# Scan beside two projections: sums moved to the transposes, relus ordered behind a cast, row loads and input parts put later

## The chip, the cores and the metric

The kernel runs on one core of one Trainium2 chip. TensorE (PE) multiplies matrices, VectorE (DVE) and ScalarE (ACT) work on vectors, GpSimd (POOL) does a little copying, and SyncE (SP) issues nearly all DMA transfers from one queue, in order. The metric is the device time of one execution in microseconds. Three runs of the kernel before the change took 2610.78 to 2611.7 us, median 2611.38.

## The reference

One layer of a hybrid encoder over 2048 frames of width 1024. Two mixers read the same normalised input. One is a short gated convolution; the other is a chunked state-space scan (SSD), with 16 heads of 64 in two groups and a state of 128. Both feed one output projection, then comes a squared-ReLU MLP and a last norm. What the change touches is the scan and the output projection:

```python
def ssd_scan(xs, dt, a_head, bm, cm):
    ...
    x_c = (xs.astype(f32) * dt[..., None]).reshape(b, nc, CHUNK, g, r, p)
    a_c = (dt * a_head).reshape(b, nc, CHUNK, g, r)
    a_cum = jnp.cumsum(a_c, axis=2)
    seg = a_cum[:, :, :, None] - a_cum[:, :, None, :]
    decay = jnp.exp(jnp.where(causal[None, None, :, :, None, None], seg, -jnp.inf))
    scores = jnp.einsum("bclgn,bcsgn->bclsg", c_c, b_c)
    y_diag = jnp.einsum("bclsgr,bcsgrp->bclgrp", scores[..., None] * decay, x_c)
    decay_end = jnp.exp(a_cum[:, :, -1:] - a_cum)
    states = jnp.einsum("bclgn,bclgrp->bcgrpn", b_c, x_c * decay_end[..., None])
    chunk_decay = jnp.exp(a_cum[:, :, -1])

    def step(hs, inp):
        s_c, d_c = inp
        return hs * d_c[..., None, None] + s_c, hs
    ...
    y_off = jnp.einsum("bclgn,bcgrpn->bclgrp", c_c, prev) * jnp.exp(a_cum)[..., None]
    return (y_diag + y_off).reshape(b, t, h, p)

def ssd_mixer(z, xbc, dt_raw, conv_w, conv_b, dt_bias, a_log, d_skip, norm_w):
    ...
    y = ssd_scan(xs, dt, a_head, bm, cm)
    y = y + d_skip.astype(jnp.float32)[:, None] * xs.astype(jnp.float32)
    y = y.reshape(b, t, SSD_INNER).astype(z.dtype)
    gated = (y * jax.nn.silu(z)).reshape(b, t, SSD_GROUPS, SSD_INNER // SSD_GROUPS)
    gated = rmsnorm(gated, norm_w.reshape(SSD_GROUPS, SSD_INNER // SSD_GROUPS))
    return gated.reshape(b, t, SSD_INNER)
    ...
    y = jnp.concatenate([y_a, y_b], axis=-1)
    x = x + jnp.einsum("btc,cd->btd", y, w_out)
```

## The kernel before

Every large product is made of three matmuls (whi by hi, whi by lo, wlo by hi): each operand is split into a rounded part (a cast on ACT) and the remainder (a subtraction on DVE). The input projection runs over two halves of 1024 frames, in pairs of column blocks, each pair as a chain of seven products (lines 246 to 290; the accumulators px, py and pw). The output projection (class Output) runs in 64 units, each one column block of 128 by one block of 512 frames, 24 matmuls into pm.

The scan takes 32 chunks of 128 frames (4 blocks, 2 groups, 4 chunks each) and is no loop of its own. It is a generator (`run`) that gives way after each step, and the projections advance it. In the first stage (16 chunks, one buffer of most tiles) one step runs after each of the seven products of the second half of the input projection. In the second stage (16 chunks, two buffers) it runs from the units of the output projection: one step in the middle of a unit, two at its end.

The work of a chunk n is in two generators.

- `front(n)`, first part: PE transposes x (ptx, L1449) and B (ptb, L1452) and multiplies B with C (L1453). ACT copies xtok (L1455) and casts btok (L1437). DVE makes xdt, masks the scores (smask) and weights xtok, and from that come the two parts of xde: the cast on ACT (L1437) and the subtraction on DVE (L1438). Second part: eight relus, one a head, over the rows dec (L1469), one exp (L1470), four multiplications of xd by the skip weight (L1472), all on ACT. Third part: DVE multiplies dec with the masked scores (L1474).
- `back(n)`, first part: PE forms the new state contribution st from btok and xde (mm3, L114 to L116), yo from the state (L1490), yd from dec and xdt (L1493). DVE updates the state (L1509, L1510) and adds yo times eb and yd (L1511, L1512). Second part: the skip term and the gate (L1514, L1515). Third: squares and their sums (ssq). Fourth: one product sums over the partitions (pss, L1524), then a square root on ACT and a reciprocal. Fifth: the scaled result is stored.

The rows come by DMA: `load(n)` fetches B and C (bc), x (xd) and dec, `load_rows(n)` fetches eb, `load_gate(n)` the gate y. dec is read by yd of the same buffer's earlier chunk, so its load waits for that product. In a chunk of the first stage nine steps are traced, in the second eight; which part stands in which step is written out by hand in `run`.

The scheduler that turns the program into queues takes instructions by program order as a priority, yet lets a later one go first where it thinks that its inputs are there earlier. `tc.issue_after` (in the helper `behind`, L100) fixes the order of two instructions of one engine; it puts no wait on the chip. PSUM banks go by tags: tp has two, yo, yd and mw one each, mm three.

In `Output`, `residual(n)` fetches the block of x to which unit n is added (xt, three buffers), and `fill` splits the inputs of the projection, for those from the scan (i = 1) with a weight (L1628 on ACT, L1629 on DVE).

Of the kernel before, what the change touches and what calls it, by code (L numbers as in the profile page):

```python
# [21 lines left out]
L = 128  # L22
# [17 lines left out]
def trunk(ctx: ExitStack, tc: tile.TileContext, x, x_tok, w_in, w_dt, w_out, w_up, w_down, cvec, hrow, out):  # L40
# [1321 lines left out]
    class Scan:  # L1362
# [5 lines left out]
        def open(self, stack, name, bufs):  # L1368
            self.sp = stack.enter_context(tc.tile_pool(name=name, bufs=1, reuse_waits="tile"))
            self.bufs = bufs  # L1370
            self.got = {}

        def tile(self, shape, tag, bufs=None):
# [10 lines left out]
        def load(self, n):  # L1384

            if n >= self.end:
                return
            b, g, c, h, ts, r0 = self.place(n)
            t = self.got[n] = {}
            if (g, c) == (0, 0) or n == self.begin:  # L1390
                dd = self.tile([4, NC * 16], "dd")
                nc.sync.dma_start(dd, dt_d[b])
                self.dd = {**getattr(self, "dd", {}), b: dd}
            t["dd"] = dd = self.dd[b]
            bc = t["bc"] = self.tile([2, L], "bc", 2)
            for i in range(2):
                nc.sync.dma_start(bc[:, i], xs_d[h][:, 8 + 2 * i + g, ts])
            t["xd"] = self.tile([4, L], "xd")
            nc.sync.dma_start(t["xd"], xs_d[h][:, 4 * g : 4 * g + 4, ts])
            t["dec"] = self.tile([HG, L], "dec")  # L1400
            nc.sync.dma_start(t["dec"], rd_d[b][r0 : r0 + HG, 0, :].partition_broadcast(P))
            three = lambda i: dd[:, i].rearrange("p (c h) -> p c h", c=NC)[:, c, g * HG : (g + 1) * HG]
            heads = lambda a: a.unsqueeze(2).to_broadcast([P, HG, 64])
            t["dt"], t["cdec"], t["dend"] = heads(three(0)), heads(three(2)), heads(three(3))
            t["a"] = dd[:, 1, r0 : r0 + HG]
            t["first"], t["last"] = (b, c) == (0, 0), (b, c) == (NB - 1, NC - 1)

        def load_rows(self, n):
# [24 lines left out]
        def pieces(self, shape, tag, src):  # L1433

            pair = self.sp.tile([P] + shape, F32R, tag=tag, name=tag, bufs=1)
            hi, lo = pair[:, 0], pair[:, 1]
            nc.scalar.copy(hi, src)  # L1437
            nc.vector.tensor_tensor(out=lo, in0=src, in1=hi.bitcast(F32), op=ALU.subtract)  # L1438
            return hi, lo

        def front(self, n):
# [12 lines left out]
            xtok = self.tile([512], "xtok", 1)  # L1454
            nc.scalar.copy(xtok, pt)  # L1455
            if not t["last"]:
                t["btok"] = self.pieces([2, P], "btok", pb[:, 0:P])
            sm = self.tile([L], "smask", 1)
            nc.vector.tensor_tensor(out=sm, in0=pb[:, P : 2 * P], in1=tri, op=ALU.mult)
# [7 lines left out]
            dec = t["dec"]  # L1467
            for i in range(HG):
                nc.scalar.activation(dec[:, i], dec[:, i], AF.Relu, bias=t["a"][:, i : i + 1], scale=-1.0)  # L1469
            nc.scalar.activation(dec, dec, AF.Exp, scale=-1.0)  # L1470
# [6 lines left out]
        def back(self, n):  # L1477
# [29 lines left out]
            else:  # L1507
                if not t["last"]:
                    nc.vector.tensor_tensor(out=byhead(state), in0=byhead(state), in1=t["cdec"], op=ALU.mult)  # L1509
                    nc.vector.tensor_tensor(out=state, in0=state, in1=st, op=ALU.add)  # L1510
                nc.vector.tensor_tensor(out=t1, in0=yo, in1=t["eb"].rearrange("p j l -> p (j l)"), op=ALU.mult)  # L1511
# [10 lines left out]
            yield  # L1522
            pss = psum("tp", "pss", 2) if self.bufs == 1 else psum("mw", "pss", accs["mw"])
            nc.tensor.matmul(pss[:, 0:L], ones, ssq, start=True, stop=True)  # L1524
# [8 lines left out]
        def run(self, begin, end):  # L1533

            self.begin, self.end = begin, end
            for n in range(begin, begin + self.bufs):
                self.load(n)
                self.load_gate(n)
                self.load_rows(n)
            yield  # L1540
            front = self.front(begin)
            for _ in front:
                yield
            if self.bufs == 1:
                for n in range(begin, end):
                    back = self.back(n)
                    front = self.front(n + 1) if n + 1 < end else iter(())
                    next(back)
                    yield
                    next(back)  # L1550
                    self.load(n + 1)
                    self.load_rows(n + 1)
                    yield
                    next(back)
                    yield
                    yield
                    next(front, None)
                    yield
                    next(back)
                    yield  # L1560
# [9 lines left out]
            for n in range(begin, end):  # L1570
# [3 lines left out]
                yield  # L1574
                next(before, None)
                yield
                next(back)
                self.load(n + 2)
                self.load_rows(n + 2)
                yield  # L1580
                next(front, None)
                yield
                if next(before, "end") != "end":
# [13 lines left out]
    class Output:  # L1597
# [19 lines left out]
        def fill(self, i, b, c, k, t):  # L1617

            blk = self.y.setdefault((i, b), {})
            for n in range(2):  # L1620
# [5 lines left out]
                if i:  # L1626
                    w = col(C_NSSD, f)
                    nc.scalar.mul(hi, o, w)  # L1628
                    nc.vector.scalar_tensor_tensor(out=lo, in0=o, scalar=w, in1=r, op0=ALU.mult, op1=ALU.subtract)  # L1629
                else:  # L1630
# [50 lines left out]
        def unit(self, n, hook):  # L1681

            i, b, d = self.UNITS[n]
            self.residual(n + 1)
            if n % 2:
# [3 lines left out]
            for k in range(KD):  # L1689
                if k == KD // 2:  # L1690
                    hook(2 * n)
                mm3(pm, whi[:, k, :], wlo[:, k, :], *self.y[i, b][k], k, KD)
            t = self.xt.pop(n)
# [179 lines left out]
```

## Time and profile before

| | |
|---|---|
| median of three runs | 2611.38 us |
| the profiled execution | 2612.25 us |
| its span, first to last instruction | 2610.1 us |
| mean granted TensorE clock | 0.998 |
| DVE busy, ACT busy | 73%, 55% |
| DMA | 533.55 MB, mean 204 GB/s |

The profile is one execution. Its rows name a line, an engine, an operation and the tiles (out<-in). A matmul's duration is longer than its share of PE's time, since matmuls overlap: from start to start a product of 512 columns takes 0.23 us. In a timeline the square bracket tells how long the engine stood still before the row and what ended that. The view of waits sums, for pairs of a waiting instruction and what released it, the microseconds, the number of times and the longest. A view of stretches gives the busy time of each engine between two times and the granted clock there.

### The profile page before, as it was taken

To read this page: it belongs to the slowest core of one execution; us is meant where nothing else is said; L and a number is where in the kernel's file an instruction comes from. 1 tells how busy PE (TensorE), PEld (TensorE's weight loads), DVE (VectorE), ACT (ScalarE), POOL (GpSimd) and SP (SyncE) were. 2 spreads that over 40 slices of the span, in tenths; PEclk is the share of its full clock that TensorE was granted. 3 is DMA by queue.
4 is the path that set the end of the run, shared out by engine and by line. 5 is a ranking of instruction groups with operands and counts; after the bars stand their busy time and mean duration, and the time that the engine had idled before them with its cause. 6 is when DMAs were issued, how large, how long until landed. Compare 5 with 4: busy or idle time off the path is not lost.

```text
span 2610.1 us, 33626 instructions
## 1 busy us (share of the span) xinstructions
PE 2591.5 (99%) x12067; PEld 2134.8 (82%) x12067; DVE 1909.7 (73%) x2625; ACT 1432.2 (55%) x2185; POOL 59.0 (2%) x98
## 2 busy tenths in 40 slices
PE   9999999999999999999999999999999999999998
PEld 7888888788888888888888888888888888888887
DVE  7988666677778777877767765755558877876875
ACT  7553345876667676766326555655456444444443
POOL 0000000000000000000000000000000000000001
PEclk9999999999999999999999999999999999999999
DMA  5657435555555488876665674643448766676872
GB/s 214 206 201 253 183 145 182 180 159 168 184 163 169 140 276 276 274 229 211 204 210 210 230 274 142 244 167 140 163 142 283 265 202 206 225 238 214 282 246 77
DMA packets 289559, 533.55 MB, mean 204 GB/s; under 512 B 25840, under 2 KB 141552, under 8 KB 289392
## 3 DMA queue, kind: packets, MB, share of 16 engines
q1 hardware_dynamic: 288816, 530.88, 60.4%
q8 instruction: 94, 1.54, 0.2%
q14 instruction: 73, 0.60, 0.1%
q10 hardware_dynamic: 576, 0.52, 0.1%
HBM read 354.63 MB, written 176.69 MB: 204 GB/s over the span
## 4 chain that ended last, share of the span: by engine, by line
PE 65%; issue 25%; DVE 4%; DMA 3%; ACT 2%; SPq 0%; POOL 0%; POOLq 0%; DVEq 0%; ACTq 0%
PE px L271 9%; PE px L273 9%; PE px L272 9%; PE py L271 5%; PE py L273 5%; PE py L272 5%; PE pm L114 4%; PE pm L116 4%; PE pm L115 4%; PE pw L271 2%; PE pw L272 2%; PE pw L273 2%; PE pm L466 1%; PE yd L1493 1%; DMA dec<-rd_d 1%
## 5 line engine op out<-in xcount | busy, mean ns | idle before, releaser
L271 PE MATMUL px<-uh,whi 128*128 128x512 f32 x1672 | 655.6, 392 | 3.8 <-DVE e L982 1.2
L273 PE MATMUL px<-uh,wlo 128*128 128x512 f32 x1672 | 651.7, 390 | 0.0
L272 PE MATMUL px<-ul,whi 128*128 128x512 f32 x1672 | 651.7, 390 | 0.0
L271 PEld LDWEIGHTS px<-uh,whi 128*128 128x128 f32 x1672 | 314.0, 188 | 74.0 <-DVE acc L1182 3.2
L273 PEld LDWEIGHTS px<-uh,wlo 128*128 128x128 f32 x1672 | 314.0, 188 | 65.6 <-issue 0.2
L106 DVE TENSOR_TENSOR wlo<-wraw,whi 128x1024 fp32r<-128x1024 f32 (+2 forms) x224 | 226.9, 1013 | 191.1 <-ACT whi L105 190.7
L272 PEld LDWEIGHTS px<-ul,whi 128*128 128x128 f32 x1672 | 314.1, 188 | 63.8
L105 ACT CAST whi<-wraw 128x1024 fp32r<-128x1024 f32 (+2 forms) x224 | 197.7, 882 | 277.6 <-PE px L272 211.1
L105 ACT CAST whi<-s 128x1024 fp32r<-128x1024 f32 (+1 forms) x206 | 215.3, 1045 | 227.8 <-PE py L272 92.5
L271 PE MATMUL py<-uh,whi 128*128 128x512 f32 x836 | 327.0, 391 | 0.0
L272 PE MATMUL py<-ul,whi 128*128 128x512 f32 x836 | 325.8, 390 | 0.0
L273 PE MATMUL py<-uh,wlo 128*128 128x512 f32 x836 | 325.8, 390 | 0.0
L106 DVE TENSOR_TENSOR wlo<-s,whi 128x1024 fp32r<-128x1024 f32 (+1 forms) x206 | 250.5, 1216 | 76.2 <-ACT whi L105 74.9
L114 PE MATMUL pm<-uh,whi 128*128 128x512 f32 (+1 forms) x584 | 226.8, 388 | 0.0
L116 PE MATMUL pm<-uh,wlo 128*128 128x512 f32 (+1 forms) x584 | 223.4, 383 | 0.0
L115 PE MATMUL pm<-ul,whi 128*128 128x512 f32 (+1 forms) x584 | 223.1, 382 | 0.0
L271 PEld LDWEIGHTS py<-uh,whi 128*128 128x128 f32 x836 | 157.0, 188 | 32.8 <-issue 0.5
L273 PEld LDWEIGHTS py<-uh,wlo 128*128 128x128 f32 x836 | 157.0, 188 | 32.6
L272 PEld LDWEIGHTS py<-ul,whi 128*128 128x128 f32 x836 | 157.1, 188 | 32.2
L326 DVE TENSOR_TENSOR ul<-rh,uh 128x1024 fp32r<-128x1024 f32 (+1 forms) x128 | 138.9, 1088 | 48.3 <-ACT uh L325 48.0
L325 ACT CAST uh<-rh 128x1024 fp32r<-128x1024 f32 (+1 forms) x128 | 119.9, 942 | 94.4 <-PE py L273 61.1
L271 PE MATMUL pw<-uh,whi 128*128 128x512 f32 x418 | 163.4, 391 | 0.0
(250 smaller groups left out, 3834.0 us busy)
## 6 DMA issues: line engine op xcount, KB each, us to landing
hid_d<-e SPq DMA_DIRECT2D x96, 512.0 KB, 4.2
rh<-hid_d SPq DMA_DIRECT2D x96, 512.0 KB, 4.6
wraw<-w_in SPq DMA_DIRECT2D x67, 512.0 KB, 4.0
wraw<-w_up SPq DMA_DIRECT2D x62, 512.0 KB, 4.3
wraw<-w_down SPq DMA_DIRECT2D x88, 256.0 KB, 4.2
dec<-rd_d SPq DMA_DIRECT2D x32, 512.0 KB, 5.4
wraw<-w_out SPq DMA_DIRECT2D x32, 512.0 KB, 4.8
x_d<-xt SPq DMA_DIRECT2D x64, 256.0 KB, 3.6
```

What stands on the lines that cost most here:

```text
L105: nc.scalar.copy(hi, raw)
L106: eng.tensor_tensor(out=lo, in0=raw, in1=hi.bitcast(F32), op=ALU.subtract)
L114: nc.tensor.matmul(out, whi, hi, start=(k == 0), stop=False)
L115: nc.tensor.matmul(out, whi, lo, start=False, stop=False)
L116: nc.tensor.matmul(out, wlo, hi, start=False, stop=(k == nk - 1))
L271: nc.tensor.matmul(p, hi, h[0], start=bool(first and k == 0), stop=False, **kw)
L272: nc.tensor.matmul(p, hi, h[1], start=False, stop=False, **kw)
L273: nc.tensor.matmul(p, lo, h[0], start=False, stop=(k == len(g) - 1), **kw)
L325: nc.scalar.copy(p[i][0], t)
L326: nc.vector.tensor_tensor(out=p[i][1], in0=t, in1=p[i][0].bitcast(F32), op=ALU.subtract)
L466: last[engine] = make(*args, **kw).ins
L1493: nc.tensor.matmul(yd[(i % 2) * 64 : (i % 2) * 64 + 64, (i // 2) * L : (i // 2 + 1) * L], byhead(t["xdt"])[:, i, :], t["dec"][:, i, :], st ...
```

## The change

In both stages the sum over the partitions (fourth part of `back`) is traced directly ahead of the transposes of the next front; in the first stage its bank is yo's and no longer one of tp's. The relus of a front are ordered behind the last cast of the front before (btok's, or the copy of xtok where there is none). The loads of a chunk are traced one step earlier; in the first stage that of x stays where it was, as a step of its own (`load_x`). In the second stage the front's first part comes a step earlier, and the first row loads (eb) stand behind the first front. In the output projection the residual of the next unit is fetched in the middle of a unit and no longer at its start, and the lower parts of the scan's outputs are ordered behind the state update traced last.

```diff
         def open(self, stack, name, bufs):
...
             self.got = {}
+            self.copied = self.updated = None
...
-            t["xd"] = self.tile([4, L], "xd")
-            nc.sync.dma_start(t["xd"], xs_d[h][:, 4 * g : 4 * g + 4, ts])
+            if self.bufs > 1 or n == self.begin:
+                self.load_x(n)
...
+        def load_x(self, n):
+
+            if n < self.end:
+                b, g, c, h, ts, r0 = self.place(n)
+                x = self.got[n]["xd"] = self.tile([4, L], "xd")
+                nc.sync.dma_start(x, xs_d[h][:, 4 * g : 4 * g + 4, ts])
...
         def pieces(self, shape, tag, src):
...
-            nc.scalar.copy(hi, src)
+            self.cast = nc.scalar.copy(hi, src).ins
...
         def front(self, n):
...
-            nc.scalar.copy(xtok, pt)
+            last, self.copied = self.copied, nc.scalar.copy(xtok, pt).ins
             if not t["last"]:
                 t["btok"] = self.pieces([2, P], "btok", pb[:, 0:P])
+                self.copied = self.cast
...
-            for i in range(HG):
-                nc.scalar.activation(dec[:, i], dec[:, i], AF.Relu, bias=t["a"][:, i : i + 1], scale=-1.0)
+            with behind(last):
+                for i in range(HG):
+                    nc.scalar.activation(dec[:, i], dec[:, i], AF.Relu, bias=t["a"][:, i : i + 1], scale=-1.0)
...
         def back(self, n):
...
-                    nc.vector.tensor_tensor(out=state, in0=state, in1=st, op=ALU.add)
+                    self.updated = nc.vector.tensor_tensor(out=state, in0=state, in1=st, op=ALU.add).ins
...
-            pss = psum("tp", "pss", 2) if self.bufs == 1 else psum("mw", "pss", accs["mw"])
+            pss = psum("yo", "pss") if self.bufs == 1 else psum("mw", "pss", accs["mw"])
...
         def run(self, begin, end):
...
-                self.load_rows(n)
+                if self.bufs == 1:
+                    self.load_rows(n)
             yield
             front = self.front(begin)
+            next(front)
+            if self.bufs > 1:
+                for n in range(begin, begin + self.bufs):
+                    self.load_rows(n)
+            yield
             for _ in front:
                 yield
             if self.bufs == 1:
...
                     next(back)
-                    yield
-                    next(back)
                     self.load(n + 1)
                     self.load_rows(n + 1)
                     yield
                     next(back)
+                    self.load_x(n + 1)
+                    yield
+                    next(back)
                     yield
                     yield
+                    next(back)
                     next(front, None)
                     yield
-                    next(back)
                     yield
                     next(front, None)
                     yield
...
                 next(back)
                 yield
-                next(before, None)
-                yield
                 next(back)
                 self.load(n + 2)
                 self.load_rows(n + 2)
                 yield
+                next(before, None)
                 next(front, None)
+                yield
                 yield
                 if next(before, "end") != "end":
                     self.load_gate(n + 1)
...
         def fill(self, i, b, c, k, t):
...
-                    nc.vector.scalar_tensor_tensor(out=lo, in0=o, scalar=w, in1=r, op0=ALU.mult, op1=ALU.subtract)
+                    with behind(scan.updated):
+                        nc.vector.scalar_tensor_tensor(
+                            out=lo, in0=o, scalar=w, in1=r, op0=ALU.mult, op1=ALU.subtract
+                        )
...
         def unit(self, n, hook):
 
             i, b, d = self.UNITS[n]
-            self.residual(n + 1)
             if n % 2:
                 self.split_weights()
...
                 if k == KD // 2:
                     hook(2 * n)
+                    self.residual(n + 1)
                 mm3(pm, whi[:, k, :], wlo[:, k, :], *self.y[i, b][k], k, KD)
```

## The prediction

> **What bounds the kernel now.** I read the page first, then the view of stretches over the two stages in which the scan runs, then the waits of TensorE (PE) there, and last the timelines around those waits.
>
> ```profile
> PE 2591.5 (99%) x12067; PEld 2134.8 (82%) x12067; DVE 1909.7 (73%) x2625; ACT 1432.2 (55%) x2185; POOL 59.0 (2%) x98
> ```
>
> PE is busy 99% of the span, and the change neither adds nor removes a matmul. So it can only win back time in which PE waits, and only between 450 and 1260 us, where the scan runs beside the projections.
>
> ```profile
> 450.00:947.00 497.00, 495.58 (x2478) 405.18 (x2477) 379.82 (x543) 348.72 (x586) 19.28 (x40) 1.00 0.55 174
> 947.00:1100.00 153.00, 153.00 (x827) 126.68 (x826) 115.96 (x185) 101.10 (x206) 0.00 (x0) 1.00 0.90 282
> 1100.00:1130.00 30.00, 28.61 (x152) 22.84 (x152) 20.42 (x33) 21.05 (x42) 0.00 (x0) 1.00 0.77 239
> 1198.00:1208.00 10.00, 8.00 (x43) 6.19 (x42) 8.58 (x16) 6.41 (x9) 0.00 (x0) 0.83 0.79 263
> ```
>
> Each row gives the stretch, its length, and the busy time of PE, its weight loads, DVE, ACT and POOL with their instructions, then the granted clock. In the first stage (450 to 947) PE stands still 1.42 us. In the second it stands still 1.39 us between 1100 and 1130 and 2.00 us between 1198 and 1208, where the granted clock is 0.83 besides; from 947 to 1100 it never does. These idle times are short of the true loss, since a busy PE can also be a slow one, so I take starts of matmuls. First a chunk that nothing disturbs, then the three disturbed ones:
>
> ```profile
> 1087.14 0.40 PE L116 MATMUL pm<-uh,wlo 128*128 128x512 f32 x1
> ...
> 1087.61 0.48 PE L115 MATMUL st<-xde,btok 128*128 128x512 f32 x1
> ...
> 1089.14 1.09 PE L1493 MATMUL yd<-dec,stmp 128*64 128x128 f32 x16
> 1090.16 0.50 PE L114 MATMUL pm<-uh,whi 128*128 128x512 f32 x1
> ```
>
> ```profile
> 1104.78 0.39 PE L116 MATMUL pm<-uh,wlo 128*128 128x512 f32 x1
> 1105.51 0.51 PE L114 MATMUL st<-xde,btok 128*128 128x512 f32 x1 [0.35 <-ACT xde L1437]
> ...
> 1109.23 0.50 PE L114 MATMUL pm<-uh,whi 128*128 128x512 f32 x1
> ```
>
> ```profile
> 1126.56 0.39 PE L116 MATMUL pm<-uh,wlo 128*128 128x512 f32 x1
> ...
> 1129.42 1.09 PE L1493 MATMUL yd<-dec,stmp 128*64 128x128 f32 x16
> ```
>
> ```profile
> 1199.47 0.39 PE L116 MATMUL pm<-uh,wlo 128*128 128x512 f32 x1
> 1201.62 0.49 PE L114 MATMUL st<-xde,btok 128*128 128x512 f32 x1 [1.77 <-ACT xde L1437]
> 1202.35 0.79 PE L115 MATMUL st<-xde,btok 128*128 128x512 f32 x1 [0.23 <-DVE xde L1438]
> ...
> 1206.42 0.50 PE L114 MATMUL pm<-uh,whi 128*128 128x512 f32 x1
> ```
>
> From the last product before the chunk (pm L116) to the first one behind it the undisturbed chunk takes 3.02 us, and 2.00 us to its yd. The others take 4.45 (1.43 lost), 2.86 to yd (0.86 lost) and 6.95 (3.93 lost): **6.22 us**. Each waits for the cast of xde on ScalarE (ACT). Why is that late?
>
> ```profile
> 1100.46 1.57 ACT L1469 ACTIVATE dec<-dec,dd 128x128 f32<-128x128 f32 x5 [6.64 <-DMA dec<-rd_d]
> ...
> 1102.23 0.57 ACT L1455 COPY xtok<-ptx 128x512 f32<-128x512 f32 x1
> ...
> 1104.85 0.61 ACT L1437 CAST xde<-xtok 128x512 fp32r<-128x512 f32 x1
> ```
>
> ```profile
> 1193.39 2.45 ACT L1469 ACTIVATE dec<-dec,dd 128x128 f32<-128x128 f32 x8 [5.41 <-DMA dec<-rd_d]
> ...
> 1200.97 0.60 ACT L1437 CAST xde<-xtok 128x512 fp32r<-128x512 f32 x1
> ```
>
> Counted from the start of the scan, eight relus a chunk, the relus here belong to the chunk after the one whose transposed inputs are copied (xtok) and cast (xde). They are ahead in ACT's queue and wait 6.64 and 5.41 us for rows (dec) that have not landed, while the transposes have long been done (1096.03, quoted below). Everything behind them on ACT is late by that.
>
> **The change part by part.**
>
> *Relus behind the cast of the chunk ahead.* The edge joins two ACT instructions, so it adds no wait, only an order: xtok and btok go ahead of the relus. Queued behind the relus stay their own exp, the cast of xde and the weight casts; DVE's subtraction for xde waits for that cast, and PE's st for both.
>
> ```profile
> L1438 DVE TENSOR_TENSOR xde<-xtok,xde 128x512 fp32r<-128x512 f32 x30 | 20.4, 681 | 3.4 <-ACT xde L1437 3.2
> ```
>
> The copy at 1102.23 can now run at about 1096.8, right behind the transposes. What can still be late is xde alone: rows at 1100.46, eight relus of 2.45, the cast of 0.61 and the subtraction of 0.68 give 1104.2; st L115 is due undisturbed at 1105.2 (1104.78 plus two products of 0.23; 1087.14 to 1087.61 holds two such). With other ACT work between, up to the 4.39 that passed from 1100.46 to 1104.85 in place of 2.45, it would be 0.9 late; I count **+0.4** between the ends 0 and 0.9. At 1199 the same sum gives 1197.2 against 1199.7. What is late next is nothing on PE. All three stalls go: **-6.2**.
>
> *Front a step earlier in the second stage.* Steps are spread over half units of twelve products (2.8 us), so transposes of two chunks in three come 2.8 us earlier and none later: more room for the same chain, no price of its own.
>
> *Sums (pss) beside the transposes.* Does a group of small matmuls cost more alone than joined?
>
> ```profile
> 1093.03 0.38 PE L1524 MATMUL pss<-ssq,ones_r 128*128 128x128 f32 x2
> ...
> 1093.48 0.40 PE L115 MATMUL pm<-ul,whi 128*128 128x512 f32 x1
> ```
>
> ```profile
> 1096.03 0.60 PE L1449 MATMUL ptx<-ident,xd 128*128 128x128 f32 x4
> ...
> 1097.03 0.39 PE L115 MATMUL pm<-ul,whi 128*128 128x512 f32 x1
> ```
>
> Less the one product of 0.23 in each stretch, two matmuls of pss cost 0.22 alone and the seven of the transposes 0.77: 0.11 each both times. So joining them is worth **0**. Against that stands only the 0.48 that the first product behind a group shows instead of 0.39; were that a price per group, 32 groups would give 2.9, which I keep as the end of the range.
>
> *The first stage's sums in bank yo.*
>
> ```profile
> ACT dec L1469 <- DMA dec<-rd_d: 51.4, 21, 6.6
> ...
> PEld ptx L1449 <- DMA xd<-xs_d: 0.8, 2, 0.4
> ...
> PEld pss L1524 <- ACT xtok L1455: 0.7, 2, 0.5
> ```
>
> Their wait for a bank (0.7 in weight loads) falls away: **-0.2**, bounds 0 and -0.7. The new wait is for DVE's product of yo, four steps (11 us) earlier in program order; queued behind the waiting pss on PE would stand the transposes and all products. The next chunk's yo in turn waits for the square root, again four steps on. Were a sum itself late, one step (2.8) is the price; no row shows PE waiting for ssq.
>
> *Input parts behind the state; residual half a unit later; row loads behind the first front; loads a step earlier.* The lower input parts (DVE) now follow the state update that was traced last; behind them stand weight parts and additions, and the first products that read them come units later. The residual load:
>
> ```profile
> L1667 SPq DMA_DIRECT2D xt<-x x32: 328/342/608, 953.7 to 1156.1; - x32
> ...
> DMA to landing us min/median/max: 2.6/3.7/8.0
> ```
>
> It keeps one and a half units, 36 products of 0.23 or 8.3 us, against a slowest landing of 8.0: **0**; without that cover it would cost the excess, under 1 us a unit. On SP it also stands less often ahead of rows, waiting for its buffer. Rows at the start of the second stage leave a stretch with no idle PE (947 to 1100): 0. The first stage's own split of its x load is a rival below.
>
> **The sum**, against the profiled execution's own 2612.25 us: -6.2 - 0.2 + 0.4 = -6.0, so 2606.2; the median of the runs, 2611.38, lies 0.87 below that execution, and I set the prediction by the median: **2605.4 us**.
>
> **The rivals.**
>
> *The relus still hold the xde cast (0.25).* The edge ends at btok; a late row then blocks xde itself. The margin computed above at 1105 is 1 us at most. If rows land 2 us later at one or two places, one stall the size of the largest returns: 2605.4 + 3.9 = 2609.3 (2606.5 to 2611.5). For it: 51.4 us of such waits in 21 places.
>
> *Order unchanged (0.08).* Relus were not the binding order, or another instruction takes their place: 2611.4.
>
> *Slower: x behind the rows in the first stage (0.12).* There x's load is issued a step after the row loads instead of among them, and a buffer of one leaves little room:
>
> ```profile
> 716.38 0.59 SPq L1424 DMA_DIRECT2D eb<-rd_d  x1
> 717.23 0.40 SPq L1399 DMA_DIRECT2D xd<-xs_d  x1
> ```
>
> ```profile
> 720.89 0.66 PE L1449 MATMUL ptx<-ident,xd 128*128 128x128 f32 x4
> ```
>
> ```profile
> 570.70 0.37 SPq L1399 DMA_DIRECT2D xd<-xs_d  x1
> ```
>
> ```profile
> 579.00 0.60 PE L1449 MATMUL ptx<-ident,xd 128*128 128x128 f32 x4
> ```
>
> ```profile
> eb<-rd_d SPq DMA_DIRECT2D x60, 128.0 KB, 4.3
> xd<-xs_d SPq DMA_DIRECT2D x32, 256.0 KB, 4.5
> ```
>
> The tightest issue to use is 3.7 us (no slack), a usual one 8.3 (3.8 of slack after a landing of 4.5). If x waited for the rows to land (4.3), the two chunks that wait today would lose 4.3 each and the thirteen others 0.5: 15.1, so 2605.4 + 15.1 = 2620.5. It decides from a shift of 3.0, where two chunks give back the 6.0. Against it: x is held by DVE's last read of its buffer, not by the queue, and the two row issues take 1.2 together.
>
> *The slow clock is not the wait's (0.05).* From st L115 to the product behind the chunk the disturbed chunk takes 4.07 us, the undisturbed 2.55: 1.52 of the 3.93 is slow clock. I put it to the 1.77 idle before it, since the stretch with shorter waits kept 1.00. Were it a dip that comes anyway, 2606.9. The Trainium skill, page "TensorE: Matmul & The Clock Gate", section "Part 1: The HAM clock gate (the "warmup" mystery)", has half rate follow an idle window of about 3.4 us. By that rule 2.0 us of idle would not be enough, and the sum would be this rival's; this trace shows the clock falling right behind 2.0 us.
>
> **How the numbers follow.** Forecast 0.50, with 2602.5 to 2607.0 for itself; rivals 0.25, 0.08, 0.12, 0.05. The range 2602.5 to 2613.0 leaves out the slower rival and the tail below the grouping's end. A measurement of this kernel tells about 0.2% (5.2 us) from no change, which puts the line at 2606.2, just above the forecast: four fifths of the forecast's case and a little of two rivals lie below it, faster 0.42; the rest of it, the held cast and the unchanged order make the same 0.45; slower 0.13.
>
> **What would show it.** No wait of st for xde over 0.3 us, and a granted clock of 1.00 throughout the scan; xtok ahead of the relus on ACT wherever rows are late; pss directly ahead of ptx at 0.11 a matmul; no new wait of ptx for x. The prediction is wrong if st waits elsewhere, if the yo bank shows up among PE's waits, or if PE waits for weights because casts moved behind the relus.

## The result, and the profile after

| | before | after |
|---|---|---|
| median of six runs each | 2611.35 us | 2620.64 us |
| lowest to highest | 2610.17 to 2613.32 | 2616.20 to 2623.84 |
| the profiled execution | 2612.25 us | 2620.62 us |
| its span | 2610.1 us | 2618.1 us |
| ratio to before | | 1.0032, 95% interval 1.0022 to 1.0043 |

By the ratio the changed kernel is 8.4 us slower (5.7 to 11.2; the medians differ by 9.3), where 6.0 faster was forecast. Of the profile after, first the line of busy times, then the same four stretches as before, with a fifth around 1190 us (length, then busy time and instructions of PE, its weight loads, DVE, ACT, POOL; granted clock; DMA share; GB/s):

```profile
PE 2593.0 (99%) x12067; PEld 2136.8 (82%) x12067; DVE 1908.3 (73%) x2625; ACT 1433.3 (55%) x2184; POOL 60.3 (2%) x98
```

```profile
450.00:947.00 497.00, 494.28 (x2475) 405.21 (x2474) 378.72 (x543) 347.11 (x584) 20.45 (x40) 1.00 0.54 172
947.00:1100.00 153.00, 150.44 (x816) 124.79 (x815) 112.48 (x180) 103.92 (x212) 0.00 (x0) 1.00 0.89 275
1100.00:1130.00 30.00, 27.94 (x142) 22.72 (x141) 22.04 (x36) 17.00 (x34) 0.00 (x0) 1.00 0.82 254
1198.00:1208.00 10.00, 10.00 (x50) 8.43 (x49) 9.00 (x17) 9.73 (x22) 0.00 (x0) 1.00 0.77 245
1188.00:1196.00 8.00, 6.32 (x30) 5.07 (x31) 4.33 (x8) 7.97 (x15) 0.00 (x0) 0.59 0.88 273
```

The stall at 1201 is gone: PE is busy throughout 1198 to 1208, at full clock. But from 947 to 1100, where PE never stood still, it now does for 2.56 us, and a stretch with the clock at 0.59 lies a little earlier instead. Where the time came from is read best by setting the same instruction of both traces side by side, here the first product (pm, L114) of a unit of the output projection:

| unit | before | after | difference | what lies between |
|---|---|---|---|---|
| 0 | 947.52 | 948.47 | +0.95 | first stage |
| 4 | 974.01 | 975.93 | +1.92 | transposes wait for x at 959 |
| 16 | 1058.87 | 1060.53 | +1.66 | |
| 20 | 1084.65 | 1088.30 | +3.65 | new: ptb waits for the state, 1079 |
| 24 | 1115.78 | 1120.36 | +4.58 | the stall at 1105 is there still, with a new one of yd |
| 28 | 1142.52 | 1146.12 | +3.60 | the stall at 1127 is gone |
| 32 | 1171.21 | 1175.26 | +4.05 | ptb waits again (0.4) |
| 36 | 1196.98 | 1207.57 | +10.59 | new: st waits for xde at 1189 |
| 40 | 1230.37 | 1236.87 | +6.50 | the stall at 1201 is gone |
| 45 | 1260.32 | 1266.90 | +6.58 | the scan has ended |

Up to the last matmul (2603.54 and 2611.54) it becomes +8.0. The part behind unit 45, which the change doesn't touch, takes from 0.5 us less to 5.8 us more in the traces of the experiments than in the trace before, so these 1.4 us tell nothing of the change. PE's waits in both stages after the change (sum, times, longest):

```profile
PE st L114 <- ACT xde L1445: 3.0, 2, 2.6
PE ptb L1460 <- DVE state L1520: 1.8, 1, 1.8
PE yd L1503 <- DVE dec L1484: 1.4, 1, 1.4
...
PE st L115 <- DVE xde L1446: 0.9, 2, 0.7
PE pss L1534 <- DVE ssq L1531: 0.9, 1, 0.9
PE ptx L1457 <- DMA xd<-xs_d: 0.8, 1, 0.8
```

Four of these six pairs are new (ptb, yd, pss, and ptx as a wait of the matmul itself). The two of st are the old ones. The largest single loss, in PE's, ACT's and SP's timelines:

```profile
1186.03 0.39 PE L116 MATMUL pm<-uh,wlo 128*128 128x512 f32 x1
1188.98 0.51 PE L114 MATMUL st<-xde,btok 128*128 128x512 f32 x1 [2.57 <-ACT xde L1445]
1190.18 0.80 PE L115 MATMUL st<-xde,btok 128*128 128x512 f32 x1 [0.69 <-DVE xde L1446]
...
1194.95 0.80 PE L114 MATMUL pm<-uh,whi 128*128 128x512 f32 x1
```

```profile
1163.78 2.45 ACT L1479 ACTIVATE dec<-dec,dd 128x128 f32<-128x128 f32 x8 [5.59 <-DMA dec<-rd_d]
...
1180.97 1.34 ACT L1645 ACTIVATE uh<-ry,cv 128x512 fp32r<-128x512 f32 x2 [6.51 <-PE pm L116]
...
1184.83 0.58 ACT L1463 COPY xtok<-ptx 128x512 f32<-128x512 f32 x1
...
1188.32 0.61 ACT L1445 CAST xde<-xtok 128x512 fp32r<-128x512 f32 x1
```

```profile
1161.16 0.58 SPq L1432 DMA_DIRECT2D eb<-rd_d  x1
1165.97 0.34 SPq L1687 DMA_DIRECT2D xt<-x  x1
1166.44 0.37 SPq L1540 DMA_DIRECT2D yn_d<-y  x1
1169.96 0.37 SPq L1439 DMA_DIRECT2D y<-sz_d  x1
...
1173.63 0.32 SPq L1687 DMA_DIRECT2D xt<-x_d  x1
1174.00 0.43 SPq L1631 DMA_DIRECT2D ry<-yn_d  x1
```

From st's predecessor to the product behind the chunk it takes 8.92 us, against 3.02 undisturbed: 5.9 lost. xde is late because ACT stands for 6.51 us ahead of two input parts (L1645), with the square root, xtok and xde queued behind. The profile names a product as releaser, but the input itself (ry), fetched only at 1174.00, landed 6.9 us later, at 1180.9, and ACT goes on at 1180.97 (such a fetch takes 6.6 here, the median between 1160 and 1190). It was fetched so late because SP's queue is in order: it stood 4.2 us before a residual load (1161.74 to 1165.97, waiting for the store that frees its buffer), then 3.2 before the gate load (waiting for the store of yn_d just ahead), then again before a residual. In the trace before, the same fetch went out at 1164.23, 9.8 us earlier, of which 4 are the distance of the two traces:

```profile
1164.23 0.37 SPq L1614 DMA_DIRECT2D ry<-yn_d  x1
```

The waits on SP between 960 and 1250, before and after:

```profile
SPq L1667 <- DMA x_d<-xt: 57.1, 35, 4.7
...
SPq L1431 <- DMA yn_d<-y: 22.1, 13, 5.5
```

```profile
SPq L1687 <- DMA x_d<-xt: 88.2, 31, 5.1
SPq L1439 <- DMA yn_d<-y: 23.6, 14, 4.3
```

The residual's wait has grown by 31 us, while others shrank: summed over all that SP waits for there, it is 166 us before and 158 after. So it isn't how long SP stands that has changed, but which loads stand behind a wait. Rows come late as well. The first row is before's, the others after's:

```profile
1092.97 0.38 SPq L1401 DMA_DIRECT2D dec<-rd_d  x1
```

```profile
1092.70 1.09 PE L1503 MATMUL yd<-dec,stmp 128*64 128x128 f32 x16
...
1099.26 0.43 SPq L1402 DMA_DIRECT2D dec<-rd_d  x1
```

Before, dec is loaded 2.74 us after the yd that frees its buffer (1090.23); after, 5.47 (1093.79). Over chunks 20 to 31 the mean went from 1.3 to 3.8 us. This delay alone doesn't order the kernels below by time: it is 1.7 us in the slowest (no_relu) and 3.0 in one that is 6 us faster than the changed kernel (no_fill). The chunk at 1109 shows what hangs on it (PE, ACT, DVE):

```profile
1109.13 0.50 PE L114 MATMUL st<-xde,btok 128*128 128x512 f32 x1 [0.47 <-ACT xde L1445]
...
1112.85 1.09 PE L1503 MATMUL yd<-dec,stmp 128*64 128x128 f32 x16 [1.37 <-DVE dec L1484]
```

```profile
1105.89 0.69 ACT L1479 ACTIVATE dec<-dec,dd 128x128 f32<-128x128 f32 x2 [6.52 <-DVE xt L1714]
...
1108.48 0.60 ACT L1445 CAST xde<-xtok 128x512 fp32r<-128x512 f32 x1
```

```profile
1110.06 0.74 DVE L1647 SCALAR_TENSOR_TENSOR ul<-ry,cv,uh 128x512 fp32r<-128x512 f32 x1
...
1110.92 0.74 DVE L1647 SCALAR_TENSOR_TENSOR ul<-ry,cv,uh 128x512 fp32r<-128x512 f32 x1
1111.58 1.22 DVE L1484 TENSOR_TENSOR dec<-dec,smask 128x1024 f32<-128x1024 f32 x1
```

ACT had xtok at 1097.45, ahead of the relus as planned; then the relus waited for rows until 1105.89 (the profile names a DVE instruction, but dec landed just then, 6.6 us behind its issue at 1099.26), and seven of the eight ran ahead of the cast of xde (1108.48). On DVE two of the lower input parts stand ahead of the product for which yd waits.

### The profile page after: what moved, and what is told of

It is laid out like the page before. It is cut to its first block, busy times and chain, and to the rows that moved or that the text cites. A ratio compares the mean times of both kernels' runs of the same rounds, so it can differ in the third digit from the quotient of the medians.

```text
span 2618.1 us, 33613 instructions
## 1 busy us (share of the span) xinstructions
PE 2593.0 (99%) x12067; PEld 2136.8 (82%) x12067; DVE 1908.3 (73%) x2625; ACT 1433.3 (55%) x2184; POOL 60.3 (2%) x98
## 4 chain that ended last, share of the span: by engine, by line
PE 39%; issue 25%; DMA 2%; ACT 1%; DVE 1%; SPq 0%; POOL 0%; POOLq 0%; DVEq 0%; ACTq 0%
PE px L271 5%; PE px L273 5%; PE px L272 5%; PE pm L114 4%; PE pm L116 4%; PE pm L115 4%; PE py L273 2%; PE py L272 2%; PE py L271 2%; PE pw L271 1%; PE pw L273 1%; PE pw L272 1%; DMA dec<-rd_d 1%; PE yd L1503 1%; PE yo L1500 1%
## 5 line engine op out<-in xcount | busy, mean ns | idle before, releaser
L114 PE MATMUL pm<-uh,whi 128*128 128x512 f32 (+1 forms) x584 | 226.2, 387 | 0.0
```

Source lines behind the costliest of these rows:

```text
L114: nc.tensor.matmul(out, whi, hi, start=(k == 0), stop=False)
```

## The experiments

Eighteen kernels, each in 5 to 12 runs, those of one group beside 23 to 35 runs of the kernel before (median 2612.5 to 2613.4). "Ratio" is to before. A trace shows one execution, which isn't always a typical one: that of relu_alone is the slowest of its twelve (2613.98), that of no_out the slowest of eleven (2621.40), that of no_first the fastest of eleven (2613.93). The times decide; a trace only shows where to look.

**Each part alone, on the kernel before.**

```diff
@@ relu_alone
-            for i in range(HG):
+            with behind(last):
+                for i in range(HG):
@@ first_alone
+            pss = psum("yo", "pss") if self.bufs == 1 ...
+                    next(back); self.load(n + 1); self.load_rows(n + 1); yield
+                    next(back); self.load_x(n + 1); yield
...
+                    next(back); next(front, None); yield
@@ second_alone
+                next(back); self.load(n + 2); self.load_rows(n + 2); yield
+                next(before, None); next(front, None); yield
@@ out_alone
+                    with behind(scan.updated):
...
+                    self.residual(n + 1)
```

> The kernel before with one part of the change: the relus ordered behind the last cast of the front before. Theory A (the loss comes from the new order of steps, and the relu edge does what it was meant to): 4 us faster than before (-2 to -6), the wait of st for xde (3.4 us in the trace of before) falls under 1 us, granted clock 1.00 at 1200. Theory B (the edge only moves the hold from the copy of xtok to the cast of xde, so the stall stays): within 1.5 us of before, st still waits 2 us or more for xde, directly behind relus that wait for rows. Theory C (the edge itself is the loss): 4 to 9 us slower.

> The kernel before with the part for the first stage alone: sums beside the transposes in the bank of yo, loads a step earlier with x left behind. Theory A: 1 to 2 us slower (the waits of pss for ssq of 0.9 and of px for the copy at 802 to 835 us, as in the trace after); nothing in the second stage. Theory C: no difference from before (within 1 us).

> The kernel before with the part for the second stage alone: sum and front one step apart, loads a step earlier, row loads behind the first front. Theory A (the new order is the main loss): 4 to 8 us slower than before, with waits of ptb for the state update (1.8 in the trace after), of ptx for the x load (0.8) and of yd for dec, and the old stall of st at about 1200 us still there. Theory C: within 1.5 us of before.

> The kernel before with the two edits of the output projection alone: lower input parts behind the state update, residual fetched half a unit later. Theory A: within 1.5 us of before. Theory D (these edits shift the queues so that an input part blocks ScalarE behind a product, 6.5 us at 1181 us in the trace after): 2 to 6 us slower, with a wait of uh L1645 for pm above 5 us on ScalarE.

| kernel | median us | ratio | interval |
|---|---|---|---|
| relu_alone | 2611.17 | 0.9987 | 0.9978 to 0.9995 |
| first_alone | 2617.90 | 1.0017 | 1.0008 to 1.0026 |
| second_alone | 2611.52 | 0.9994 | 0.9985 to 1.0003 |
| out_alone | 2614.75 | 1.0005 | 0.9997 to 1.0014 |

The relu edge is worth 3.4 us alone (though its profiled execution, the slowest, still has 4.0 us of waits of st for xde), the first stage's part costs 4.4, more than theory A's 1 to 2, the two others nothing that can be told apart. Theory C falls, and A has the sign right for the relus and the first stage only: the second stage's order, which was to be the main loss, costs nothing by itself. The longest stall left in relu_alone's trace, 2.2 us, is theory B's (ACT):

```profile
1219.40 0.98 ACT L1478 ACTIVATE dec<-dec,dd 128x128 f32<-128x128 f32 x3 [7.05 <-DMA dec<-rd_d]
1220.30 0.60 ACT L1444 CAST xde<-xtok 128x512 fp32r<-128x512 f32 x1
```

The trace of out_alone has a new wait of yd for dec, 1.4 us. Multiplied, the four give 1.0003; the changed kernel has 1.0032. So some parts cost only together.

**One part undone, from the changed kernel.** The edits are those above, taken back.

```diff
@@ no_first, no_second, no_relu, no_out: e.g. no_relu
-            with behind(last):
-                for i in range(HG):
+            for i in range(HG):
```

> The changed kernel without the part for the first stage. Changed stood at 1.0032 of before; the parts alone gave 0.9987 (relus), 1.0017 (first stage), 0.9994 (second stage), 1.0005 (output projection), which multiply to 1.0003. Theory A (the first stage's part is the loss and carries over whole): 1.0015 of before (2 to 6 us less than the changed kernel), no wait of pss for ssq, none of px for the copy at 800 to 850 us. Theory F (the loss is a coincidence of late transfers in the second stage, which any part can set off): 1.0000 to 1.0010, and a trace without the stall of st at 1186 us.

> The changed kernel without the part for the second stage. Theory A: 1.0035 (nothing won, since that part alone lost nothing). Theory G (with the second stage's new order SyncE's queue runs two round trips one after the other, store of x_d to load of xt, then store of yn_d to load of the gate, and everything behind them, rows and inputs, comes late): 1.0005 to 1.0015, no wait of ptb for the state update.

> The changed kernel without the order of the relus. Theory A: 1.0045 (the edge wins 3 us there as it did alone), with the copy of xtok behind relus that wait for rows. Theory H (in the new order the edge is worth nothing, as the transposes come earlier and xtok stands ahead of the relus anyway): 1.0032, as the changed kernel, within 1.5 us.

> The changed kernel without the two edits of the output projection. Theory A: 1.0027. Theory D (these edits bring the late input parts that block ScalarE ahead of the cast of xde): 1.0010 to 1.0018, and no stall of st above 1.5 us behind an input part.

| kernel | median us | ratio | interval |
|---|---|---|---|
| no_first | 2617.22 | 1.0014 | 1.0005 to 1.0022 |
| no_second | 2617.09 | 1.0015 | 1.0007 to 1.0024 |
| no_relu | 2623.49 | 1.0041 | 1.0029 to 1.0053 |
| no_out | 2615.93 | 1.0009 | 0.9999 to 1.0019 |

The first stage (1.7 to 1.8 parts in a thousand lost) counts the same in both directions. So do the relus (1.3 won alone, 0.9 in the changed kernel), but the intervals of no_relu, five runs, and of the changed kernel overlap, so 0.9 can't be told from nothing. The second stage's order costs 1.7 in a thousand and the edits of the output projection 2.3 when taken from the changed kernel (each give or take 1.4), though neither did alone: the pair is the second loss. In no_first and no_out st still waited some 2 us near 1183, behind input parts, against theories F and D. In no_second no ptb waits for the state, as theory G has it, but yd waits 3.3 us for dec.

**Which half of the output projection's edits; and SP's queue.**

```diff
@@ no_resid: back at the start of unit(n); no_fill: no edge
+            self.residual(n + 1)
...
-                    with behind(scan.updated):
@@ after_resid_pool, before_resid_pool: in residual(n)
-                nc.sync.dma_start(t, x[b, :, d] if i == 0 else x1_d[b][:, d])
+                nc.gpsimd.dma_start(t, x[b, :, d] if i == 0 else x1_d[b][:, d])
```

> The changed kernel with the residual fetched at the start of a unit again. Eight variants so far fit one term: the second stage's order and the edits of the output projection cost about 0.0027 (7 us) only where both are there. Theory Q (the residual is the half of it: traced half a unit later it stands in SyncE's queue just ahead of what the new order of the second stage put there, and its wait for the store of its buffer, 88 us in all in the changed kernel against 57 before, delays rows and inputs): 1.0005 to 1.0015 of before, the wait of the residual for the store back under 75 us, the issue of dec less than 2.5 us behind the yd that frees its buffer (3.8 in the changed kernel, 1.3 before). Rival I (the input parts are the half of it): 1.0032 as the changed kernel.

> The changed kernel without the order of the lower input parts behind the state update. Theory Q: 1.0032 as the changed kernel, within 1.5 us. Rival I (lower parts behind the state update hold the stores and the fetches of inputs that wait for them, so an input part blocks ScalarE ahead of the cast of xde): 1.0005 to 1.0015.

> The changed kernel with the residual loads of the output projection issued from GpSimd's queue instead of SyncE's, so that their waits for a store delay nothing else. Theory Q: 4 to 10 us less than the changed kernel (0.9995 to 1.0015 of before), dec issued less than 2 us behind the yd that frees it, no stall of st behind an input part at about 1186 us. Rival J (what costs is the position of the fronts on TensorE and the bank they share with st, not SyncE's queue): within 2 us of the changed kernel, 1.0025 to 1.0040, the wait of ptb for the state update of 2 us still there.

> The kernel before with the residual loads issued from GpSimd's queue. Theory Q: these waits (57 us on SyncE) delay rows here too, if less: 2 to 6 us faster than before (0.9977 to 0.9992), the waits of st for xde under 1.5 us in all. Rival J: within 1.5 us of before.

| kernel | median us | ratio | interval |
|---|---|---|---|
| no_resid | 2620.02 | 1.0029 | 1.0015 to 1.0043 |
| no_fill | 2613.66 | 1.0008 | 0.9999 to 1.0017 |
| after_resid_pool | 2610.20 | 0.9990 | 0.9982 to 0.9999 |
| before_resid_pool | 2615.00 | 1.0008 | 0.9999 to 1.0017 |

Theory Q is half wrong: it isn't the new place of the residual (SP waited 87.5 us for it in no_resid too), it is the order of the lower input parts (rival I). Without it the product that yd waits for goes ahead of xde's subtraction, with no lower part near it, and yd waits nowhere:

```profile
1102.64 1.22 DVE L1484 TENSOR_TENSOR dec<-dec,smask 128x1024 f32<-128x1024 f32 x1
1104.09 0.69 DVE L1446 TENSOR_TENSOR xde<-xtok,xde 128x512 fp32r<-128x512 f32 x1 [0.23 <-ACT xde L1445]
```

Yet no_fill keeps the stall behind the inputs (1.9 at 1183). The other half of theory Q, that the residual's loads on SP are what makes rows and inputs late, holds for the changed kernel: with these loads on GpSimd's queue it is 11 us (4.2 in a thousand) faster, dec goes out 0.5 us after its yd, and of all waits of PE behind 963 us none is left, the one of ptb for the state included; rival J falls. (One of ptx for x stays at 962.6, 2.4 us.) On the kernel before the same move won nothing, and dec came no earlier (1.8 us after its yd, for 1.3). SP's waits don't tell why: in both kernels with the move it stands 46.2 us before the gate (22.1 and 23.6 without), and in all longer than without it (181 and 185 us, for 166 and 158). So that the move helps the changed kernel is shown; why it brings dec forward there and not in the kernel before is open.

**The halves of the first stage; the pair alone; all that helps together.**

```diff
@@ first_sum: the sum's step moved, bank of yo; first_sum_tp: the same, bank of tp
+                    next(back)
                     next(front, None)
                     yield
-                    next(back)
                     yield
@@ first_loads: load, load_rows and load_x moved, sum where it was
@@ second_fill: second_alone with the edge of the lower parts
@@ best_pool: the changed kernel less its first-stage part, less that edge,
   with the residual on GpSimd's queue
```

> The kernel before with half of the first stage's part: the sums beside the transposes, in the bank of yo; loads where they were. Theory K (the sum comes a step earlier than its input is ready: pss waits 0.9 us for ssq at about 836 us, and the products around it slip): 2 to 5 us slower than before, 1.0008 to 1.0019, with that wait of 0.9. Rival L (the loads are the half that costs): within 1.5 us of before, no wait of pss for ssq over 0.5.

> The kernel before with the other half of the first stage's part: B, C, dec and eb loaded a step earlier, x left behind as a step of its own; sums where they were, in a bank of tp. Rival L: 2 to 5 us slower, 1.0008 to 1.0019, with the waits of the projection at 802 and 832 us and a longer wait of ptx for x at about 960 us. Theory K: within 1.5 us of before.

> The kernel before with the second stage's part and the lower input parts ordered behind the state update, nothing else. Theory M (these two together are what costs about 7 us: with the fronts earlier, the lower parts that are held back until the state update stand on VectorE directly ahead of the product of dec that yd waits for, and the fetches of inputs behind them come late): 1.0010 to 1.0025, a wait of yd for dec over 1 us. Rival N (it takes the relu edge or the residual as well): 0.9990 to 1.0003.

> The changed kernel without its first-stage part and without the order of the lower input parts, and with the residual loads from GpSimd's queue. If the costs add as the runs so far say (first stage 0.0017, residual waits on SyncE 0.0042 of the changed kernel, of which the lower parts' order may be a part): 0.9965 to 0.9980 of before, no stall of st, yd or ptb above 0.5 us in the second stage, dec issued less than 1 us behind the yd that frees it. If the lower parts' order and GpSimd's queue cure the same loss: 0.9973 to 0.9985. If the first stage's loss was only the start of the second stage: 0.9985 to 0.9995.

> The same half of the first stage's part (sums beside the transposes on the kernel before, 1.0015), but in a bank of tp as before. If the step is what costs (the sum is asked for a step earlier, before its input): 1.0008 to 1.0022, the wait of pss for ssq of 0.8 to 0.9 still there. If the bank of yo is what costs: 1.0000 to 1.0005.

| kernel | median us | ratio | interval |
|---|---|---|---|
| first_sum | 2617.93 | 1.0015 | 1.0006 to 1.0024 |
| first_loads | 2613.06 | 1.0000 | 0.9991 to 1.0009 |
| second_fill | 2616.71 | 1.0013 | 1.0004 to 1.0023 |
| best_pool | 2607.14 | 0.9975 | 0.9966 to 0.9985 |
| first_sum_tp | 2620.99 | 1.0028 | 1.0020 to 1.0037 |

The sums are the first stage's loss, the loads are free (theory K). In first_sum the trace shows it at one place:

```profile
833.94 0.44 PE L1456 MATMUL ptx<-ident,xd 128*128 128x128 f32 x2
835.17 0.46 PE L1532 MATMUL pss<-ssq,ones_r 128*128 128x128 f32 x2 [0.79 <-DVE ssq L1529]
```

The same instructions of its trace and before's move apart by 2.5 us from 785 to 974; the median's 3.9 has 1.6 to 6.3 as interval. The place repeats: between the products that stand at 820 and 840 us in the trace before, the eleven traces with the sums moved lose 1.3 to 2.0 us, the eight without -0.2 to 0.6. Where the rest of the 3.9 lies isn't shown. In a bank of tp it measured 3.4 us more, above both expected ranges (though the two intervals overlap): there ptb waits for the square root that empties the bank (2.1 us in four places, the longest below), which the bank of yo avoids.

```profile
870.89 0.33 PE L1459 MATMUL ptb<-ident,bc 128*128 128x128 f32 x1 [1.11 <-ACT ssq L1534]
```

second_fill adds 1.9 in a thousand to second_alone, with yd waiting for dec 3.3 us in two places: the pair is enough (theory M). That wait isn't the pair's alone, though: six of the nine traces with the edge of the lower parts have yd wait for dec (1.1 to 3.4 us in all), out_alone and no_second among them, which lack the second stage's order, and none of the eleven without the edge. So it is the edge that brings the wait; that it costs time only with that order is what the ratios suggest, but the intervals (out_alone -0.3 to 1.4 in a thousand, second_fill 0.4 to 2.3) overlap. best_pool beats both kernels, by 6.5 us (3.9 to 8.9) the kernel before. Its stretches:

```profile
1100.00:1130.00 30.00, 30.00 (x167) 25.05 (x166) 19.14 (x30) 17.26 (x31) 3.23 (x6) 1.00 0.73 212
1198.00:1208.00 10.00, 10.00 (x65) 8.46 (x64) 8.78 (x17) 4.52 (x14) 0.54 (x1) 1.00 0.82 272
...
1200.00:1250.00 50.00, 50.00 (x263) 41.58 (x260) 35.09 (x56) 21.53 (x41) 4.30 (x8) 1.00 0.50 166
```

PE stands nowhere in the three places of the prediction. Unit 45 begins at 1254.13, against 1260.32 before: 6.19 us earlier, of which 1.72 come between units 20 and 24, 0.98 between 24 and 28 and 4.09 between 36 and 40, where the prediction counted 1.43, 0.86 and 3.93. The kernel's ratio lies in the first two of the three expected ranges, so it doesn't decide between them. Since after_resid_pool less the first stage's loss comes out the same (0.9990 less 0.0015 to 0.0018), the lower parts' edge seems to cost nothing once the residual loads are off SP's queue; it was not tried by itself.

**The relus behind the cast of xde.**

```diff
                 t["xde"] = self.pieces([2, 512], "xde", xtok)
+                self.copied = self.cast
```

> The changed kernel with the relus ordered behind the cast of xde instead of that of btok. Rival 1 of the prediction (relus that wait for rows hold the cast of xde): the wait of st for xde (3.0 and 0.9 us in the changed kernel) falls by 1 to 2 us at about 1109 us; what the late rows then hold is the product of dec, so yd waits for it as long or longer (1.4 before). In all 0 to 3 us less than the changed kernel, 1.0020 to 1.0032 of before. If the input parts and not the relus hold ScalarE, no change: 1.0032.

Ratio 1.0019 (1.0009 to 1.0028), median 2618.13. The stall at 1109 is gone, and against the expectation no wait of yd took its place. The one at 1189 stayed (2.0 and 0.9 us lost in starts): so relus without rows held xde at the first place, inputs at the second.

## Why the prediction was wrong

Between the forecast (6.0 faster) and the measurement (8.4 slower) lie 14.4 us. Three steps failed, and by the runs they make some 11 to 14 of these, an estimate from the ratios above, each term give or take 2 to 4 us: the stalls that did not go (5.8 expected, 2.4 to 3.4 won), the sums that were taken for free (3.9), and the lower input parts that were taken for free (5 to 6).

- **Relus behind the cast (-6.2 + 0.4).** The size of the stalls was right: best_pool takes 6.19 us off at unit 45. The failed step is "All three stalls go", with "What is late next is nothing on PE". Alone the edge won 3.4 us: it ends at btok, and a late row then holds xde itself (relu_alone at 1219), as the first rival said at 0.25. In the changed kernel one of three places was cleared, one stayed (1109) and one was replaced by another of the same kind a chunk earlier (1189, 5.9 us with the slow clock). What was next was the input part on ACT, late for the same reason as the rows: their place in SP's queue.
- **Sums beside the transposes (0, end of the range 2.9).** Cost: 3.9 us (1.6 to 6.3), the largest loss that stands alone. The seven matmuls cost no more joined; the failed step is "no row shows PE waiting for ssq". The sum is asked for a step earlier, and whether its input is there could be read in the trace before:

```profile
835.73 0.66 PE L1449 MATMUL ptx<-ident,xd 128*128 128x128 f32 x4
```

```profile
835.51 0.28 DVE L1521 TENSOR_TENSOR ssq<-stmp 128x128 f32<-128x128 f32 x1
```

  ssq ends at 835.79, behind the start of the transposes ahead of which the sum was to go. Of the first stage's chunks it is the tightest; in the others ssq is ready 0.45 us or more ahead of them. The row alone would give a wait of 0.06; in first_sum the transposes also stand four products earlier on PE, and it is 0.79. The prediction named the mechanism and its price (one step, 2.8) and then took zero.
- **Bank of yo (-0.2).** Right in kind; in the new order the bank of tp measured 3.4 us more, if only just clear of noise.
- **Front a step earlier ("no price of its own").** Wrong by one place. ptb needs the bank that st holds until the state update:

```profile
1079.71 0.33 PE L1460 MATMUL ptb<-ident,bc 128*128 128x128 f32 x1 [1.78 <-DVE state L1520]
```

  Seven of the nine kernels with this order and the residual on SP wait there about 1 to 3 us, the others 0.4 and 0.7; the two with the residual on GpSimd not at all, so it too hangs on what SP brings late. Alone the order cost no time (second_alone, 0.9994).
- **Lower input parts behind the state (0).** The failed step is "behind them stand weight parts and additions". Behind them stood the product of dec, which yd waits for. With the second stage's order this costs 1.9 (second_fill over second_alone) to 2.4 in a thousand (the changed kernel over no_fill), 5 to 6 us, give or take 4; out_alone, without it, measured 0.5 (-0.3 to 1.4).
- **Residual half a unit later (0).** Right for the time (no_resid 1.0029), wrong in its reason: SP stands before it not less but longer, 88.2 us for 57.1.
- **Slower by x behind the rows in the first stage.** Right side, wrong mechanism: first_loads measured 1.0000.
- **The clock.** In the changed kernel it fell behind the new long wait (0.59 from 1188 to 1196) and no longer at 1201, as the forecast had it; no dip came by itself in the places of before.
- **Two slips in the sum at 1199** change nothing: its terms give 1197.1 and not 1197.2, and 1199.7 counts one product of 0.23 where 1105.2 counts two (1199.9).

## What to carry over

When a step is moved ahead, look up in the old trace when its input is ready at the new place, in the chunk where that is tightest; one such row decides more than any price per instruction. Where a stall ends at a late transfer, look at the queue that issues it: in the changed kernel an edge between instructions that wait for the transfer mostly chose which of them was late, and moving one kind of load to another queue won 11 us. In the kernel before the same move won nothing, so it has to be tried. Price parts in pairs where they share an in-order queue: here two whose cost alone was within noise cost 5 to 6 us together, and with the residual on another queue and the sums left where they were the forecast gain came back.

## What the runs showed of the hardware

The granted clock falls behind idle times of 1.3 to 2.6 us, but not behind each. In first_sum 1.88 us idle is followed by 3.4 us at 0.50; in after_xde_edge 2.36 us leave it at 1.00 (each a row of PE's timeline, then the stretch behind it). Before the last products of the kernel the twenty traces have fourteen such times at half rate; twelve last 3.41 us and two twice that, so a stretch's 0.59 or 0.83 is a mean of 0.50 and 1.00:

```profile
1203.34 0.72 PE L114 MATMUL st<-xde,btok 128*128 128x512 f32 x1 [1.88 <-ACT xde L1444]
```

```profile
1203.46:1206.86 3.40, 3.39 (x11) 2.53 (x11) 2.89 (x4) 2.69 (x3) 0.00 (x0) 0.50 0.81 280
```

```profile
1083.27 0.33 PE L1460 MATMUL ptb<-ident,bc 128*128 128x128 f32 x1 [2.36 <-DVE state L1521]
```

```profile
1084.00:1090.00 6.00, 6.00 (x28) 4.96 (x27) 6.00 (x12) 3.31 (x10) 0.00 (x0) 1.00 1.01 288
```

The Trainium skill, page "TensorE: Matmul & The Clock Gate", section "Part 1: The HAM clock gate (the "warmup" mystery)", has half rate follow an idle window of about 3.4 us, counted in windows that run freely. That the same idle time counts at one moment and not at another fits windows of that kind, and so does the length of the times at half rate; that a whole window has to be idle does not, since no single idle time here reaches 3.4 us.

The stalls that hang on a late transfer differ from trace to trace, so one trace shows a sample of them. The runs spread by several us for every kernel: 7.6 us in the six of the changed one, 9.3 to 10.0 in the 23 to 35 of the kernel before.
